# Six modulation vectors of two layers: from matrix products to sums of products along rows

## The chip, the cores and the metric

The kernel runs on one core of a Trainium2 chip. The metric is the device time of one launch in microseconds. The engines are named as the profile names them: PE is TensorE (PEld its weight loads), DVE is VectorE, ACT is ScalarE, POOL is GpSimd, and SP is SyncE, which only issues DMAs here.

## What is computed

Two blocks follow each other. The first has two layers of a mixer (window attention, forgetting attention, a state-space part) and an attention to a memory; the second has two layers of another mixer and a mixture of experts, both modulated by a condition. Only the making of that modulation changes:

```python
def _adaln(cond, w, b):
    return jnp.matmul(jax.nn.silu(cond), w) + b

def _modulate(h, shift, scale):
    return h * (1 + scale) + shift

# second block, layer l of 2; c is [1, 1024], c_ctx [1024], w_mod[l] [1024, 6144]
m_lat = jnp.split(_adaln(c, w_mod[l], b_mod[l])[:, None, :], N_MOD, axis=-1)   # N_MOD = 6
m_ctx = jnp.split(_adaln(c_ctx, w_mod[l], b_mod[l]), N_MOD, axis=-1)
h = _modulate(_rmsnorm(x, norm1_w[l]), m_lat[0], m_lat[1])
```

So for two conditions and two layers a vector of 1024 numbers is multiplied by a matrix of 1024 x 6144 floats, 24 MB a layer. Neither the conditions nor the weights depend on anything that the kernel computes: the work can be done at any time before the second block needs it.

## The kernel before

Features lie on the 128 partitions, tokens along the row. A weight tile of 128 output columns and 1024 inputs is loaded by SP into `wr` (two buffers), split into a high and a low half by ACT (L460, `wh`) and DVE (L462, `wl`, three buffers each), and multiplied in three passes on PE (L472 to L474, into `psg`, two banks). `steps` (L506) runs the tiles of one matrix and hands each result to a callback; after each tile it calls `aside`.

Layer l of the first block is `mixer1` (46 tiles of the input matrix and 16 of the output matrix, between them the scores, softmaxes, convolution and state space) and `memory1` (32 tiles). The trace has layer 0 up to 709 us and layer 1 up to 1450 us; the second block follows.

The modulation is a side line, `adaln`, a generator that `aside` advances. `mixer1` starts it behind its window attention (L736), once in each layer, for that layer's weights; every second tile advances it by two. A step loads 512 KB of weights into `wm` (two buffers of 4 KB a partition) and issues four matmuls on PE, whose stationary operand is silu of the two conditions, padded to 32 columns (`cs`, made in `consts2`), each into another strip of 32 rows of the bank `psa`. After sixteen steps ACT copies the bank (L1078), PE transposes it (L1081) and DVE adds the bias into `mod` (L1082). A layer has 48 steps.

A scheduler orders the instructions of each engine: it takes what is ready by its own estimate of time, in the order of the program where several are ready, and gives out the buffers. Each engine then runs its queue in order and waits at semaphores. An instruction that waits holds up all that stands behind it on its engine.

Of the kernel before, what the change touches and what calls it, by code (L numbers as in the profile page):

```python
# [16 lines left out]
OP = mybir.AluOpType  # L17
# [3 lines left out]
P = 128  # L21
# [163 lines left out]
def _layout2(g, A, vec, cst):  # L185
# [1 line left out]
    cst.update(d)  # L187
    A.update(cp)
    A["ctx_in"] = g["ctx_2"][0]
    vec["cc"] = np.ascontiguousarray(  # L190
        np.stack([_cols(g["c_2"][0]), _cols(g["c_ctx_2"])], 2).reshape(P, 16))
    lb = g["hg_lb_logits_2"]
    vec["lbl"] = np.concatenate([_cols(lb[d_, l]) for l in range(2) for d_ in range(2)], 1)
    for l in range(DEPTH):
# [6 lines left out]
        A[f"v_o{l}0"] = _pieces(g["w_out_2"][l][:384], 2)  # L201
        A[f"v_o{l}1"] = _pieces(g["w_out_2"][l][768:], 2)
        A[f"v_o{l}2"] = _pieces(g["w_out_2"][l][384:768], 2)
        A[f"wm{l}"] = np.ascontiguousarray(
            g["w_mod_2"][l].reshape(8, P, 3, 4, 2, 256).transpose(2, 4, 0, 1, 3, 5).reshape(48, P, 1024))
        A[f"rpb{l}"] = _rpb(g["na_rpb_2"][l])
        wr = np.concatenate([g["w_router_2"][l], np.zeros((D, 16), w.dtype)], 1)
        A[f"wr{l}"] = np.ascontiguousarray(wr.reshape(KT, P, 32).transpose(1, 0, 2).reshape(P, -1))
# [26 lines left out]
class _K:  # L235
    def __init__(self, ctx, tc, A, off, boff):
        self.tc, self.nc, self.A = tc, tc.nc, A
        self.n = self.ns = 0
        self.off, self.boff = off, boff
        self.packs = {}  # L240
        self.queue, self.early = [], []
        self.side, self.due = iter(()), 0
        e = ctx.enter_context
        self.pools = {"one": e(tc.tile_pool(name="p_one", bufs=1)),
                      "y": e(tc.tile_pool(name="p_y", bufs=8, reuse_waits="tile"))}
        self.ps = e(tc.tile_pool(name="ps", bufs=1, space=PSUM))
        self.ps_bufs = {"g": 2, "s": 2, "t": 2, "o": 1, "a": 1}
# [245 lines left out]

    def aside(self):

        self.due += 1
        if self.due % 2 == 0:
            for _ in range(2):
                next(self.side, None)

    def until(self, g):

# [85 lines left out]
    def mixer1(self, l, x, ps, rb):  # L588
# [144 lines left out]
            vec.scalar_tensor_tensor(y, po, 0.5, ga[j], OP.mult, OP.mult)  # L733
            y0.append(self.hilo(y, "y"))

        self.side = self.adaln(l)  # L736

        kq = []

# [298 lines left out]
    def consts2(self):  # L1038
        nc, A = self.nc, self.A
        self.hm = self.one("hm", [P, 5 * 32], U8)  # L1040
        hm = self.tl("t", [P, 512])[:, :5 * 32]
        nc.sync.dma_start(hm, A["hmask"])
        nc.vector.tensor_copy(self.hm, hm)

        cc = self.v("cc").rearrange("p (k v) -> p k v", v=2)
        th = self.sm("cth", [P, 8, 2])
        nc.scalar.activation(th, cc, AF.Tanh, scale=0.5)
        hc = self.sm("chf", [P, 8, 2])
        nc.vector.tensor_scalar(hc, cc, 0.5, None, OP.mult)
        self.cs = self.one("cs", [P, 8, 32])  # L1050
        nc.vector.memset(self.cs, 0.0)
        nc.vector.scalar_tensor_tensor(self.cs[:, :, :2], th, 1.0, hc, OP.add, OP.mult)

        lbl = self.v("lbl")
        self.lb = self.one("lb", [P, 2, 6])
        nc.vector.tensor_tensor(self.lb[:, 0], lbl[:, :6], lbl[:, 6:], OP.subtract)
        nc.vector.tensor_tensor(self.lb[:, 1], lbl[:, 6:], lbl[:, :6], OP.subtract)
        nc.scalar.activation(self.lb, self.lb, AF.Exp)
        nc.vector.tensor_scalar(self.lb, self.lb, BIG, 1.0, OP.min, OP.add)
        nc.vector.reciprocal(self.lb, self.lb)  # L1060
        self.mod = [self.one(f"mod{l}", [P, 6, 8, 2]) for l in range(DEPTH)]

    def adaln(self, l):

        nc = self.nc
        bm = self.v(f"bm{l}")
        for s in range(3):
            ps = self.pt("a")
            for n in range(16):
                hf, k = n // 8, n % 8  # L1070
                raw = self.tl("wm", [P, 1024])
                nc.sync.dma_start(raw, self.A[f"wm{l}"][s * 16 + n])
                for j in range(4):
                    nc.tensor.matmul(ps[32 * j:32 * j + 32, hf * 256:hf * 256 + 256], self.cs[:, k],
                                     raw[:, j * 256:(j + 1) * 256], start=k == 0, stop=k == 7)
                yield
            row = self.tl("t", [P, 512])
            nc.scalar.activation(row, ps, AF.Copy)  # L1078
            pq = self.pt("a")
            for b in range(4):  # L1080
                nc.tensor.transpose(pq[:, b * P:(b + 1) * P], row[:, b * P:(b + 1) * P], self.idf)  # L1081
            nc.vector.tensor_tensor(  # L1082
                self.mod[l][:, 2 * s:2 * s + 2].rearrange("p m (h b) v -> p (m h) b v", h=2),
                pq.rearrange("p (b j r) -> p j b r", b=4, j=4)[:, :, :, :2],
                bm[:, 16 * s:16 * s + 16].rearrange("p (j b) -> p j b", j=4)[:, :, :, None].to_broadcast([P, 4, 4, 2]),
                OP.add)

    def mod_cols(self, l, v, n, w):

# [743 lines left out]
def tile_body(ctx, tc, A, off, boff, out):  # L1833
# [3 lines left out]
    K.consts()  # L1837
    x = K.one("x", [P, KT, T])
    cx = K.one("cx", [P, KT, 256])
    with K.scope(wr=2, wh=3, wl=3, t=6, tg=3, h=16, f2=24, ac=2, xc=2, wm=2, sm=2, s1=1):  # L1840
        ss = K.s1("ssx", [P, 8])
        K.to_feat(A["x"], 4, x, "f2", ss)
        K.consts1()
        nc.vector.tensor_tensor(ss[:, :4], ss[:, :4], ss[:, 4:], OP.add)
        rb = K.row_of(K.rsqrt(ss[:, :4], 4, 1.0 / D), 4)
        K.consts2()
        ps = None
        for l in range(DEPTH):
            mT, ps = K.mixer1(l, x, ps, rb)
# [1 line left out]
                K.to_feat(A["ctx_in"], 2, cx, "f2")  # L1851
            rb = None
            (ps, *pw), hcT = K.memory1(l, x, mT, ps, cx)
            for _ in K.side:
                pass
        rb = K.final_norm([ps, *pw]), hcT
    K.block2(x, cx, rb, dram, out)

# [19 lines left out]
```

## Time and profile before

| | us |
|---|---|
| median of three runs (lowest to highest) | 3010.46 (3009.3 to 3012.07) |
| the profiled execution | 3010.19 |
| its span, first to last instruction | 3007.3 |
| PE busy in the span | 2794.3 |
| DVE, ACT, POOL busy | 1532.0, 1198.2, 278.6 |

Times of rows count from the start of the span. Busy time is the time in which at least one instruction of an engine runs; its instructions overlap a little at their ends, so the durations of single instructions add up to somewhat more. A row of groups gives line, engine, operation, tiles and shape, count, busy us, mean ns, and the idle time ahead of it with what ended that. Tiles are named by the program without their numbers: `wl<-wr,wh` writes `wl` from `wr` and `wh`.

### The profile page before, as it was taken

The numbers are of one execution on the slowest core, as the hardware profiler recorded it, in microseconds if no ns is written. First come the engines' busy times: TensorE is split into PE (matmuls) and PEld (weight loads), VectorE is DVE, ScalarE is ACT, GpSimd is POOL, SyncE is SP. The second block draws the span as 40 slices with busy tenths as digits, with TensorE's granted clock in tenths as the row PEclk, the third lists the DMA queues.
The fourth block names the chain that finished last, engine by engine and source line by source line (L and its number), as shares of the span: only waits on it lengthen the run. The fifth ranks groups of instructions, "written<-read, shape, count | busy, mean of one in ns | idle before, by whom it ended". The sixth has DMA issues, their size and how long they took to land. (4 is left out here: it accounts for less than half of the span.)

```text
span 3007.3 us, 46731 instructions
## 1 busy us (share of the span) xinstructions
PE 2794.3 (93%) x18975; PEld 1932.1 (64%) x18976; DVE 1532.0 (51%) x3103; ACT 1198.2 (40%) x2466; POOL 278.6 (9%) x276
## 2 busy tenths in 40 slices
PE   7999999999999999999999999989996999997975
PEld 5777767876777767877776877733334767773321
DVE  4655786544565686636456556721115365574100
ACT  4545354443554454434455243331112463443110
POOL 0000031000100030100011011011111010001101
PEclk9999999999999999999999999989997999998999
DMA  4232425412222424421110110589974111129997
GB/s 135 64 133 92 168 99 175 152 59 70 77 99 106 140 97 163 167 93 40 54 39 22 58 44 27 226 338 378 372 287 121 63 34 55 52 73 358 409 404 301
DMA packets 97574, 439.53 MB, mean 146 GB/s; under 512 B 11216, under 2 KB 12496, under 8 KB 72784
## 3 DMA queue, kind: packets, MB, share of 16 engines
q1 hardware_dynamic: 86976, 401.09, 36.2%
q0 software_dynamic: 9520, 32.32, 4.0%
q8 instruction: 149, 2.44, 0.3%
q10 hardware_dynamic: 864, 3.15, 0.3%
q14 instruction: 65, 0.53, 0.1%
HBM read 416.40 MB, written 20.97 MB: 145 GB/s over the span
## 5 line engine op out<-in xcount | busy, mean ns | idle before, releaser
L472 PE MATMUL psg<-h,wh 128*128 128x512 f32 x1616 | 652.0, 404 | 2.4 <-ACT z L1345 1.9
L474 PE MATMUL psg<-h,wl 128*128 128x512 f32 x1616 | 646.2, 400 | 0.0
L473 PE MATMUL psg<-h,wh 128*128 128x512 f32 x1616 | 644.3, 399 | 0.0
L462 DVE TENSOR_TENSOR wl<-wr,wh 128x1024 fp32r<-128x1024 f32 (+2 forms) x272 | 339.9, 1250 | 432.9 <-ACT wh L460 418.2
L460 ACT ACTIVATE wh<-wr 128x1024 fp32r<-128x1024 f32 (+2 forms) x272 | 280.8, 1033 | 515.1 <-PE psg L473 440.8
L472 PEld LDWEIGHTS psg<-h,wh 128*128 128x128 f32 x1616 | 305.6, 189 | 88.9 <-issue 20.7
L474 PEld LDWEIGHTS psg<-h,wl 128*128 128x128 f32 x1616 | 305.5, 189 | 71.5 <-issue 9.8
L473 PEld LDWEIGHTS psg<-h,wh 128*128 128x128 f32 x1616 | 305.6, 189 | 68.1 <-issue 7.9
L1750 PE MATMUL psg<-ew,xg 128*64 128x512 f32 x832 | 221.6, 605 | 23.0 <-DMA ew<-in_eu_dram 12.2
L472 PE MATMUL psg<-y,wh 128*128 128x256 f32 (+1 forms) x560 | 182.1, 326 | 1.3 <-ACT y L448 0.6
L473 PE MATMUL psg<-y,wh 128*128 128x256 f32 (+1 forms) x560 | 181.1, 324 | 1.9 <-DVE y L449 1.9
L474 PE MATMUL psg<-y,wl 128*128 128x256 f32 (+1 forms) x560 | 180.0, 323 | 0.2 <-DVE wl L462 0.2
L1750 PEld LDWEIGHTS psg<-ew,xg 128*64 128x64 f32 x832 | 65.0, 138 | 154.4 <-issue 112.1
L472 PEld LDWEIGHTS psg<-y,wh 128*128 128x128 f32 x560 | 108.7, 195 | 15.1 <-DVE x L1101 2.0
L472 PE MATMUL psg<-f,wh 128*128 128x256 f32 (+1 forms) x360 | 113.2, 316 | 4.0 <-DVE x L582 1.8
L473 PEld LDWEIGHTS psg<-y,wh 128*128 128x128 f32 x560 | 108.4, 194 | 11.5 <-DVE y L449 2.2
L1030 ACT ACTIVATE t<-pst 128x512 f32<-128x512 f32 (+1 forms) x134 | 69.6, 557 | 110.9 <-PE pst L1027 110.6
L473 PE MATMUL psg<-f,wh 128*128 128x256 f32 (+1 forms) x360 | 112.8, 314 | 0.8 <-DVE f L1265 0.8
L474 PEld LDWEIGHTS psg<-y,wl 128*128 128x128 f32 x560 | 108.8, 195 | 6.6 <-issue 0.6
L474 PE MATMUL psg<-f,wl 128*128 128x256 f32 (+1 forms) x360 | 111.6, 310 | 0.0
L1777 PE MATMUL pss<-ew,hid 128*64 128x512 f32 x400 | 106.3, 597 | 4.2 <-DMA ew<-in_ed_dram 4.2
L1027 PE MATMUL pst<-const_sb,t 128*128 128x128 f32 x488 | 83.3, 280 | 6.3 <-DVE t L1255 4.5
(475 smaller groups left out, 4525.5 us busy)
## 6 DMA issues: line engine op xcount, KB each, us to landing
ew<-in_eg_dram SPq DMA_DIRECT2D x52, 1024.0 KB, 15.0
ew<-in_eu_dram SPq DMA_DIRECT2D x52, 1024.0 KB, 9.8
ew<-in_ed_dram SPq DMA_DIRECT2D x50, 1024.0 KB, 10.2
wm<-in_wm_dram SPq DMA_DIRECT2D x96, 512.0 KB, 4.1
wr<-in_w_f_dram SPq DMA_DIRECT2D x92, 512.0 KB, 3.6
wr<-in_v_f_dram SPq DMA_DIRECT2D x60, 512.0 KB, 3.3
wr<-in_w_o_dram SPq DMA_DIRECT2D x32, 512.0 KB, 5.0
x<-in_ed_dram SPq DMA_DIRECT2D x10, 1024.0 KB, 16.8
```

The costliest lines, as they stand in the source:

```text
L460: nc.scalar.activation(hi, raw, AF.Copy)
L462: nc.vector.tensor_tensor(lo, raw, hi, OP.subtract)
L472: t.matmul(ps, a[0], b[0], start=first, stop=False)
L473: t.matmul(ps, a[0], b[1], start=False, stop=False)
L474: t.matmul(ps, a[1], b[0], start=False, stop=last)
L1027: ten.transpose(pp[:, (2 * i + a) * P:(2 * i + a + 1) * P], ps[a][:, c:c + P], self.idf)
L1030: self.nc.scalar.activation(pT[:, :w], pp[:, :w], AF.Copy)
L1750: ten.matmul(ps[e * 64:(e + 1) * 64], x0[:, d, e * 64:(e + 1) * 64], wn[e][:, k], start=d == 0, stop=d == 7)
L1777: ten.matmul(ps[e * 64:(e + 1) * 64], hid[0, q][:, f, e * 64:(e + 1) * 64], w[j][e][:, f], start=f == 0, stop=f == 3)
```

## The change

The weights of the modulation are transposed on the host: 48 tiles a layer, in which a partition holds one output and the row half of its 1024 weights (512 floats, 256 KB a tile). The two conditions are stored 128 times over, once for each partition. `adaln` now runs once, over both layers. For each half it loads the conditions (`csb`) and makes their silu with ACT and GpSimd. A step loads one tile into `wm` (three buffers of 2 KB, for the tile `w` and for a product `q`); GpSimd multiplies it by the silu of the second condition into `q`, ACT sums `q` along the row, and DVE multiplies by the first condition, over `w` itself, and sums in one instruction. The sums land in `part`; DVE adds the halves and the bias at the end of a layer's second half. There are 192 steps; `aside` advances one at every tile, from the first tile of layer 0 on. The pool `f2` of feature tiles has 23 buffers instead of 24. PE, its bank `psa` and the transposes are not used by the modulation any more.

```diff
--- before.py
+++ after.py
@@ -187,8 +187,7 @@
     cst.update(d)
     A.update(cp)
     A["ctx_in"] = g["ctx_2"][0]
-    vec["cc"] = np.ascontiguousarray(
-        np.stack([_cols(g["c_2"][0]), _cols(g["c_ctx_2"])], 2).reshape(P, 16))
+    A["cc"] = _bc(np.stack([g["c_2"][0], g["c_ctx_2"]], 0).reshape(2, 2, 512).transpose(1, 0, 2).reshape(-1))
     lb = g["hg_lb_logits_2"]
     vec["lbl"] = np.concatenate([_cols(lb[d_, l]) for l in range(2) for d_ in range(2)], 1)
     for l in range(DEPTH):
@@ -201,8 +200,7 @@
         A[f"v_o{l}0"] = _pieces(g["w_out_2"][l][:384], 2)
         A[f"v_o{l}1"] = _pieces(g["w_out_2"][l][768:], 2)
         A[f"v_o{l}2"] = _pieces(g["w_out_2"][l][384:768], 2)
-        A[f"wm{l}"] = np.ascontiguousarray(
-            g["w_mod_2"][l].reshape(8, P, 3, 4, 2, 256).transpose(2, 4, 0, 1, 3, 5).reshape(48, P, 1024))
+        A[f"wm{l}"] = np.ascontiguousarray(g["w_mod_2"][l].T.reshape(48, P, 2, 512).transpose(2, 0, 1, 3))
         A[f"rpb{l}"] = _rpb(g["na_rpb_2"][l])
         wr = np.concatenate([g["w_router_2"][l], np.zeros((D, 16), w.dtype)], 1)
         A[f"wr{l}"] = np.ascontiguousarray(wr.reshape(KT, P, 32).transpose(1, 0, 2).reshape(P, -1))
@@ -239,7 +237,7 @@
         self.off, self.boff = off, boff
         self.packs = {}
         self.queue, self.early = [], []
-        self.side, self.due = iter(()), 0
+        self.side = iter(())
         e = ctx.enter_context
         self.pools = {"one": e(tc.tile_pool(name="p_one", bufs=1)),
                       "y": e(tc.tile_pool(name="p_y", bufs=8, reuse_waits="tile"))}
@@ -493,10 +491,7 @@
 
     def aside(self):
 
-        self.due += 1
-        if self.due % 2 == 0:
-            for _ in range(2):
-                next(self.side, None)
+        next(self.side, None)
 
     def until(self, g):
 
@@ -733,7 +728,6 @@
             vec.scalar_tensor_tensor(y, po, 0.5, ga[j], OP.mult, OP.mult)
             y0.append(self.hilo(y, "y"))
 
-        self.side = self.adaln(l)
 
         kq = []
 
@@ -1042,15 +1036,6 @@
         nc.sync.dma_start(hm, A["hmask"])
         nc.vector.tensor_copy(self.hm, hm)
 
-        cc = self.v("cc").rearrange("p (k v) -> p k v", v=2)
-        th = self.sm("cth", [P, 8, 2])
-        nc.scalar.activation(th, cc, AF.Tanh, scale=0.5)
-        hc = self.sm("chf", [P, 8, 2])
-        nc.vector.tensor_scalar(hc, cc, 0.5, None, OP.mult)
-        self.cs = self.one("cs", [P, 8, 32])
-        nc.vector.memset(self.cs, 0.0)
-        nc.vector.scalar_tensor_tensor(self.cs[:, :, :2], th, 1.0, hc, OP.add, OP.mult)
-
         lbl = self.v("lbl")
         self.lb = self.one("lb", [P, 2, 6])
         nc.vector.tensor_tensor(self.lb[:, 0], lbl[:, :6], lbl[:, 6:], OP.subtract)
@@ -1060,30 +1045,33 @@
         nc.vector.reciprocal(self.lb, self.lb)
         self.mod = [self.one(f"mod{l}", [P, 6, 8, 2]) for l in range(DEPTH)]
 
-    def adaln(self, l):
+    def adaln(self):
+
 
         nc = self.nc
-        bm = self.v(f"bm{l}")
-        for s in range(3):
-            ps = self.pt("a")
-            for n in range(16):
-                hf, k = n // 8, n % 8
-                raw = self.tl("wm", [P, 1024])
-                nc.sync.dma_start(raw, self.A[f"wm{l}"][s * 16 + n])
-                for j in range(4):
-                    nc.tensor.matmul(ps[32 * j:32 * j + 32, hf * 256:hf * 256 + 256], self.cs[:, k],
-                                     raw[:, j * 256:(j + 1) * 256], start=k == 0, stop=k == 7)
-                yield
-            row = self.tl("t", [P, 512])
-            nc.scalar.activation(row, ps, AF.Copy)
-            pq = self.pt("a")
-            for b in range(4):
-                nc.tensor.transpose(pq[:, b * P:(b + 1) * P], row[:, b * P:(b + 1) * P], self.idf)
-            nc.vector.tensor_tensor(
-                self.mod[l][:, 2 * s:2 * s + 2].rearrange("p m (h b) v -> p (m h) b v", h=2),
-                pq.rearrange("p (b j r) -> p j b r", b=4, j=4)[:, :, :, :2],
-                bm[:, 16 * s:16 * s + 16].rearrange("p (j b) -> p j b", j=4)[:, :, :, None].to_broadcast([P, 4, 4, 2]),
-                OP.add)
+        part = self.s1("adp", [P, DEPTH, 2, 2, 48])
+        for h in range(2):
+            cs = self.s1("csb", [P, 2, 512])
+            nc.sync.dma_start(cs, self.A["cc"][:, h * 1024:(h + 1) * 1024].rearrange("p (v k) -> p v k", v=2))
+            for v in range(2):
+                th = self.tl("wm", [P, 512])
+                nc.scalar.activation(th, cs[:, v], AF.Tanh, scale=0.5)
+                nc.gpsimd.tensor_tensor(th, th, cs[:, v], OP.mult)
+                nc.gpsimd.tensor_tensor(th, th, cs[:, v], OP.add)
+                nc.scalar.activation(cs[:, v], th, AF.Copy, scale=0.5)
+            for l in range(DEPTH):
+                for n in range(48):
+                    w, q = self.tl("wm", [P, 512]), self.tl("wm", [P, 512])
+                    nc.sync.dma_start(w, self.A[f"wm{l}"][h, n])
+                    nc.gpsimd.tensor_tensor(q, w, cs[:, 1], OP.mult)
+                    nc.scalar.activation(q, q, AF.Copy, accum_out=part[:, l, h, 1, n:n + 1])
+                    nc.vector.tensor_tensor_reduce(w, w, cs[:, 0], 1.0, 0.0, OP.mult, OP.add, part[:, l, h, 0, n:n + 1])
+                    yield
+                if h:
+                    m = self.mod[l].rearrange("p m k v -> p v (m k)")
+                    bm = self.v(f"bm{l}")[:, None, :].to_broadcast([P, 2, 48])
+                    nc.vector.tensor_tensor(m, part[:, l, 0], part[:, l, 1], OP.add)
+                    nc.vector.tensor_tensor(m, m, bm, OP.add)
 
     def mod_cols(self, l, v, n, w):
 
@@ -1837,13 +1825,14 @@
     K.consts()
     x = K.one("x", [P, KT, T])
     cx = K.one("cx", [P, KT, 256])
-    with K.scope(wr=2, wh=3, wl=3, t=6, tg=3, h=16, f2=24, ac=2, xc=2, wm=2, sm=2, s1=1):
+    with K.scope(wr=2, wh=3, wl=3, t=6, tg=3, h=16, f2=23, ac=2, xc=2, wm=3, sm=2, s1=1):
         ss = K.s1("ssx", [P, 8])
         K.to_feat(A["x"], 4, x, "f2", ss)
         K.consts1()
         nc.vector.tensor_tensor(ss[:, :4], ss[:, :4], ss[:, 4:], OP.add)
         rb = K.row_of(K.rsqrt(ss[:, :4], 4, 1.0 / D), 4)
         K.consts2()
+        K.side = K.adaln()
         ps = None
         for l in range(DEPTH):
             mT, ps = K.mixer1(l, x, ps, rb)
@@ -1851,8 +1840,8 @@
                 K.to_feat(A["ctx_in"], 2, cx, "f2")
             rb = None
             (ps, *pw), hcT = K.memory1(l, x, mT, ps, cx)
-            for _ in K.side:
-                pass
+        for _ in K.side:
+            pass
         rb = K.final_norm([ps, *pw]), hcT
     K.block2(x, cx, rb, dram, out)
```

What the scheduler makes of it differs from the order in the program. DVE at the first output matrix of layer 0, before (L582 adds a result to `x`, L462 makes a low half):

```order
L462 TENSOR_TENSOR wl_1775<-wr_1771,wh_1773 128x1024
L582 TENSOR_TENSOR x<-x,psg_1697 128x512
L582 TENSOR_TENSOR x<-x,psg_1711 128x512
L462 TENSOR_TENSOR wl_1964<-wr_1960,wh_1962 128x1024
L582 TENSOR_TENSOR x<-x,psg_1731 128x512
L582 TENSOR_TENSOR x<-x,psg_1745 128x512
L462 TENSOR_TENSOR wl_2019<-wr_2015,wh_2017 128x1024
```

The same place on DVE now (L460 is the low half, L577 the addition, L1068 the product and its sum, two instructions):

```order
L460 TENSOR_TENSOR wl_2047<-wr_2043,wh_2045 128x1024
L1068 ISA wm_4098,adp_381<-wm_4098,csb_382 128x512
L1068 ISA adp_381 128x1
L577 TENSOR_TENSOR x<-x,psg_1814 128x512
L1068 ISA wm_4138,adp_381<-wm_4138,csb_382 128x512
L1068 ISA adp_381 128x1
L577 TENSOR_TENSOR x<-x,psg_1828 128x512
L460 TENSOR_TENSOR wl_2096<-wr_2092,wh_2094 128x1024
```

Two products stand between one low half and the next, each ahead of an addition. Counted over the whole order, 16 products stand ahead of the twelfth of the 272 low halves, 80 between that and the 45th, none up to the 48th, 39 up to the 72nd, 52 up to the 96th and 5 behind it; the 94th is the last of layer 0. In the trace of before the 12th, 45th, 48th, 72nd and 96th start at 92, 369, 416, 565 and 709 us.

PE at the same output matrix, before (L1074 are the matmuls of the modulation):

```order
L473 MATMUL psg_1651<-y_1457,wh_1647 128x512
L474 MATMUL psg_1651<-y_1456,wl_1649 128x512
L1074 MATMUL psa_1503<-wm_1679,cs 32x256 x4
L1074 MATMUL psa_1503<-wm_1685,cs 32x256
L472 MATMUL psg_1665<-y_970,wh_1647 128x512
L473 MATMUL psg_1665<-y_971,wh_1647 128x512
```

And now, between the first and the second result of that matrix:

```order
L471 MATMUL psg_1734<-y_1541,wh_1730 128x512
L472 MATMUL psg_1734<-y_1540,wl_1732 128x512
L566 MATMUL pss_1894<-f_368_1578,f_376_1625 128x128
L470 MATMUL psg_1748<-y_1036,wh_1730 128x512
L471 MATMUL psg_1748<-y_1037,wh_1730 128x512
L472 MATMUL psg_1748<-y_1036,wl_1732 128x512
```

The matmuls of the modulation are gone from the row of the others; one of the scores (L566) stands there.

## Rows read from the trace of the kernel before

**Rows 1.** The page: busy us, share of the span and instructions by engine.
```profile
PE 2794.3 (93%) x18975; PEld 1932.1 (64%) x18976; DVE 1532.0 (51%) x3103; ACT 1198.2 (40%) x2466; POOL 278.6 (9%) x276
```

**Rows 2.** Windows: length; PE, PEld, DVE, ACT, POOL busy (records); clock, DMA, GB/s.
```profile
92.00:369.00 277.00, 273.39 (x1658) 202.79 (x1658) 178.53 (x377) 133.73 (x299) 8.58 (x21) 1.00 0.34 116
369.00:416.00 47.00, 43.72 (x342) 31.31 (x342) 43.80 (x83) 27.20 (x72) 15.14 (x13) 1.00 0.20 70
416.00:565.00 149.00, 146.94 (x926) 116.88 (x927) 104.59 (x174) 69.23 (x122) 19.52 (x14) 1.00 0.46 157
565.00:709.00 144.00, 141.17 (x695) 112.43 (x694) 57.65 (x108) 56.76 (x126) 0.00 (x0) 1.00 0.29 94
625.00:677.00 52.00, 49.73 (x203) 34.09 (x202) 25.50 (x77) 24.24 (x79) 0.00 (x0) 1.00 0.12 41
709.00:1240.00 531.00, 513.41 (x3016) 378.60 (x3015) 336.63 (x633) 250.08 (x515) 50.20 (x51) 0.99 0.33 112
```

**Rows 3.** Waits from 92 to 565 us: total, times, longest, of two engines.
```profile
DVE wl L462 <- ACT wh L460: 46.8, 36, 4.9
...
ACT wh L460 <- PE psg L473: 84.0, 40, 5.6
```

**Rows 4.** Windows of the modulation's matmuls (tile wm) alone: length; PE, PEld busy.
```profile
92.00:369.00 277.00, 16.83 (x224) 6.19 (x224) 1.00 0.34 116
369.00:416.00 47.00, 2.75 (x32) 0.96 (x32) 1.00 0.20 70
416.00:565.00 149.00, 9.18 (x128) 3.46 (x128) 1.00 0.46 157
709.00:1240.00 531.00, 30.40 (x384) 10.68 (x384) 0.99 0.33 112
```

**Rows 5.** Timeline of TensorE around one group: start, duration, line.
```profile
170.38 1.07 PE L1074 MATMUL psa<-wm,cs 128*32 128x256 f32 x16
171.38 0.50 PE L472 MATMUL psg<-h,wh 128*128 128x512 f32 x1
```

**Rows 6.** Groups of DVE from 92 to 565 us: busy us, mean ns, idle before.
```profile
L863 DVE SCALAR_TENSOR_TENSOR f<-f,f 128x512 f32<-128x512 f32 x8 | 5.5, 690 | 0.2
L826 DVE TENSOR_TENSOR t<-t,t 128x512 f32<-128x512 f32 x16 | 15.2, 951 | 0.4 <-ACT t L825 0.2
L855 DVE TENSOR_TENSOR f<-f,ends 128x512 f32<-128x512 f32 x4 | 4.6, 1147 | 0.0
L828 DVE COPY ends<-t 128x4 f32<-128x4 f32 x16 | 5.7, 354 | 0.0
```

**Rows 7.** Groups of GpSimd from 92 to 565 us.
```profile
L830 POOL TENSOR_TENSOR t<-t,f 128x512 f32<-128x512 f32 x12 | 17.6, 1467 | 23.7 <-ACT t L825 8.6 <-DVE ends L828 8.5 <-ACT wh L460 5.4
L875 POOL TENSOR_TENSOR x<-x,tg 128x512 f32<-128x512 f32 x8 | 10.3, 1291 | 93.0 <-DVE tg L874 93.0
L846 POOL TENSOR_TENSOR t<-f,dst 128x512 f32<-128x512 f32 x6 | 6.7, 1121 | 11.7 <-PE pso L839 6.3 <-PE pss L849 3.0 <-DVE f L801 2.4
```

**Rows 8.** Timelines of GpSimd and of DVE at one place.
```profile
499.80 1.29 POOL L875 TENSOR_TENSOR x<-x,tg 128x512 f32<-128x512 f32 x1 [5.75 <-DVE tg L874]
...
499.94 2.23 DVE L462 TENSOR_TENSOR wl<-wr,wh 128x1024 fp32r<-128x1024 f32 x1 [0.23 <-ACT wh L460]
```

**Rows 9.** Lines of DVE with min/median/max ns; the mean of one of them.
```profile
L462 DVE TENSOR_TENSOR wl<-wr,wh x272: 681/1226/2351, 19.4 to 2710.2; 128x1024 fp32r<-128x1024 f32 x124, 128x768 fp32r<-128x768 f32 x8, 128x512 fp32r<-128x512 f32 x4
...
L828 DVE COPY ends<-t x32: 154/164/952, 371.7 to 1131.9; 128x4 f32<-128x4 f32 x32
...
L462 DVE TENSOR_TENSOR wl<-wr,wh 128x1024 fp32r<-128x1024 f32 x61 | 82.3, 1349 | 48.7 <-ACT wh L460 46.8 <-PE pst L799 0.8 <-PE psg L474 0.6
```

**Rows 10.** Groups of ACT to 60 us: a square with its sum, and the sum's read.
```profile
L360 ACT ACTIVATE tg<-f 128x512 f32<-128x512 f32 x8 | 5.0, 621 | 4.3 <-DMA f<-in_x_dram 4.3
L360 ACT ACTIVATION_READ_ACCUMULATOR tg<-f 128x1 f32 x8 | 1.5, 190 | 0.0
```

**Rows 11.** DMA issues: KB each, median us to landing.
```profile
wr<-in_v_o_dram SPq DMA_DIRECT2D x8, 256.0 KB, 2.5
```

## The prediction

> **What bounds the kernel now.** I read the page first, then the windows of the two layers of the first block, then the single rows. TensorE is busy 93% of the span [rows 1]. [...] Next comes DVE: 178.53 + 43.80 + 104.59 = 327 of 473 us (69%), in the 47 us from 369 to 416 already 43.80 (93%) [rows 2]. Its longest wait is for the high halves of the weights, 46.8 us, and ACT waits 84.0 us for TensorE to give those buffers back [rows 3]. That idle time is prefetch held back by a full buffer, so it can absorb some work, not all. GpSimd works 43 us there [rows 2]. From 1240 us on nothing is touched.
>
> **What leaves TensorE.** The 768 records of the modulation lie half in each layer and cover 28.76 us (16.83 + 2.75 + 9.18) and 30.40 us [rows 4]. Against one group: its 16 records start at 170.38, the matmul behind them at 171.38 us; 48 groups of 1.00 us are 48 us [rows 5]. So 48 to 59 us leave TensorE; I take 59, which has the switches in it and the groups that are split. The 24 transposes behind them, at the 0.06 us of one record, are 1.5 us; I leave them out.
>
> **Where the new work lands.** It doesn't stay where the old was. The order puts 16 of the 192 steps ahead of the twelfth low half of the weights (92 us in the trace), 80 from there to 369, none to 416, 39 to 565, 52 to 709 and 5 later. Layer 1 thus loses its modulation and gets nothing for it, while layer 0 takes nearly all.
>
> **DVE in layer 0.** A 128x512 product of two SBUF tensors takes 0.69 us [rows 6]. The read of its sum lies between nothing and the 0.164 us of the smallest copy [rows 9]; part of it lies beside the next product. I take 0.7 us a step: 178.53 + 80 x 0.7 = 234.5 us in the 277 us to 369, 43.8 in the next 47, 104.59 + 39 x 0.7 = 131.9 in the 149 to 565 [rows 2]. TensorE without its modulation would want 260, 44 and 140 us [rows 2, 4]. By this alone DVE still fits, at 90 to 99%.
>
> **What GpSimd takes from DVE.** This decides. A two-tensor product of 128x512 takes GpSimd 1.29 us [rows 7]. At 499.80 us one starts, and the DVE subtraction that starts at 499.94 takes 2.23 us, where 1.226 is its median [rows 8, 9]. So a DVE instruction that reads two SBUF tensors stands while GpSimd reads two. [...] From the rows: 61 subtractions at 1349 instead of 1226 ns make 7.5 us over eight L875 products, 0.94 us each [rows 7, 9]. Beside the 18 products of L830 and L846, DVE lost (951-690) x 16 + (1147-690) x 4 + (354-164) x 16 = 9.0 us, 0.5 each [rows 6, 7, 9]. The new rows stand nearer to the first: the product of DVE overwrites the weights that GpSimd reads, so it waits for GpSimd, and the subtractions behind it stand in the same queue. I take 0.7, with 0.5 and 0.94 as ends. To 369 that is 234.5 + 56 = 290.5 us (274.5 to 309.7) for 277; to 565 131.9 + 27.3 = 159.2 (151.4 to 168.6) for 149. Sum with the 47: 497 for 473, +24 us (0 to +52).
>
> DVE never runs without gaps: its fullest stretch is 93% busy [rows 2]. At 93%, 290.5 becomes 312 and 159.2 becomes 171, +58 us (+32 to +88). I take the middle between no gap and that, **+40 us in layer 0** instead of the 29 it should have gained. Queued behind a late product on DVE are the low halves, the softmax steps and the additions that free TensorE's PSUM buffers, so TensorE waits for what stands behind it.
>
> **The rest.** From 565 to 709 us DVE has 57.65 us [rows 2]; 52 x 1.4 = 73 fit. Only the softmax of the memory from 625 to 677 is dense: 25.50 + 20 x 1.4 = 53.5 us for 52 [rows 2]. I put +3 us (0 to +8). ACT gets 0.62 + 0.19 us a step [rows 10], at most 119 x 0.81 = 96 us on 133.73 + 27.20 + 69.23 = 230 of 473 [rows 2]: 69%, hidden by its waits for TensorE's buffers, and if those are gone its sums come late and hold the buffer of the next step. SP issues 192 loads of 256 KB where it issued 96 of 512 KB; the same bytes; 256 KB need 2.5 us to land [rows 11]. They wait for a buffer ahead of the loads of the weights, but two steps need 2.5 + 1.29 + 0.81 us, 4.6, and have eight (473/119 each). On GpSimd the products and casts of the attention now stand behind new ones that wait for their load; with 119 x 1.29 + 43 = 197 of 473 us it is free more than half of the time, so I charge nothing, up to 1.29 us at each of its 26 products, those of DVE's waits above among them [rows 2, 7]. One buffer fewer in the pool of features: no row shows a wait on it; I take nothing, up to 6 us as for the longest wait on a weight buffer, 5.6 [rows 3].
>
> **Sum.** Layer 0 +40 and +3, layer 1 -30: +13 us on the profiled 3010.2 us, **3023 us**; the median 3010.46 is the same to 0.3 us. Its own range is 2983 (0.5 us a product, no gaps) to 3080 (0.94 us at 93%, the softmax at +8, layer 1 at 26 instead of 30).
>
> **Rivals.**
> *The cover holds.* DVE's waits for the high halves shrink instead, and the products of GpSimd fall where DVE waits anyway. From 0.3 us a product downwards (234.5 + 80 x 0.3 = 258.5 under the 260 of TensorE) most of layer 0's 29 us comes too: 3010 - 59 = 2951 in full, 2980 if layer 0 only breaks even. For it: DVE has 146 us of idle time, and its longest total of waits is for buffers that are full [rows 3]. Against it: no stretch of DVE above 93%. 31%.
> *The fused sum is slow.* No row of this trace multiplies and sums on DVE. Bounds are 0.69 us, a plain product, and 1.23 us, the subtraction of twice the width [rows 6, 9]. At 1.23, 119 x 0.54 = 64 us more in a layer where DVE has no room: 3087, up to 3130 with 0.94 us. For it speaks only that the sum is one more thing to do; the plain product of that width costs 0.69. 12%. [...]
> *Layer 1 gives nothing*, because what TensorE then waits for takes the place: DVE is at 336.63 of 531 us there [rows 2], so I give it 7%, at 3040 to 3053.
>
> The forecast has 50%. Of it some 9 in 50 lie within 0.2% (6 us, about what a measurement of this kernel can tell from no change) and 3 below; of the first rival three in 31 lie within. So faster 0.31, same 0.12, slower 0.57. The range leaves out the fullest form of the first rival (2951 to 2960) and the end of the second: 2960 to 3095.
>
> **What would show it.** Subtractions (the low halves) with a mean over 1.5 us in layer 0; products of DVE waiting for GpSimd; TensorE idle for 40 to 80 us between 92 and 620 us in place of 9, with waits on DVE; layer 1 some 30 us shorter than its 531. Wrong: TensorE as full as before in layer 0 and that layer shorter (cover), fused products over 1 us (second rival), or layer 1 as long as before.

## The result and the profile after

The changed kernel takes **3066.44 us** (median of four runs, 3062.84 to 3069.0) against 3011.24 (3009.3 to 3012.07) in the same comparison: a ratio of 1.0179, 95% interval 1.0166 to 1.0191. The forecast was 3023 in a range from 2960 to 3095, slower at 57%. The sign and the ranges hold; the loss is 55 us (56 between the spans of the profiled executions) where the sum had 13.

Lines of the changed kernel are two to twelve lower than before: L460 makes the low half (L462 before), L458 the high half, L470 to L472 multiply. New are L1066 (GpSimd's product), L1067 (ACT's sum) and L1068 (DVE's product and sum). The page's row of busy time and instructions, to be held against [rows 1]:

```profile
PE 2754.6 (90%) x18184; PEld 1919.1 (63%) x18184; DVE 1743.2 (57%) x3482; ACT 1321.6 (43%) x2851; POOL 575.4 (19%) x476
```

Windows of the changed kernel from the 12th to the 72nd low half, on to the 96th, and to the 160th (length; PE, PEld, DVE, ACT, POOL busy; granted clock, DMA, GB/s). The same pieces of work were 92 to 565, 565 to 709 and 709 to 1241 us before, [rows 2] but for 1 us:

```profile
99.00:623.00 524.00, 450.81 (x2529) 347.18 (x2528) 455.78 (x857) 306.84 (x729) 232.31 (x172) 0.97 0.40 125
623.00:788.00 165.00, 147.84 (x702) 115.96 (x701) 112.27 (x216) 90.49 (x230) 70.97 (x53) 0.97 0.52 164
788.00:1296.00 508.00, 480.73 (x2617) 369.17 (x2617) 342.80 (x647) 250.63 (x523) 54.24 (x56) 0.97 0.21 71
```

The first stretch begins 7 us later and takes 524 us for 473, the memory's 165 for 144, layer 1 takes 508 for 532: +7 + 51 + 21 - 24, and 1 us more behind that. TensorE, idle for 9 us in the first stretch before, is idle for 73. It waits less for DVE (33 us in all) than for ACT (40). Waits of TensorE from 99 to 623 us (total, times, longest):

```profile
PE pss L811 <- ACT t L804: 12.0, 2, 10.0
PE psg L470 <- ACT xc L771: 8.8, 6, 2.0
PE pst L1021 <- DVE t L1009: 7.8, 9, 1.6
PE pst L362 <- ACT cx L366: 7.2, 2, 6.8
```

ACT in turn waits for GpSimd, and so does DVE. Waits of ACT and of DVE in the same stretch; before, the longest of ACT was 84.0 us, for TensorE to free a weight buffer, and that of DVE 46.8 us, for ACT's high halves [rows 3]:

```profile
ACT wm L1067 <- POOL wm L1066: 83.3, 67, 3.7
ACT wh L458 <- PE psg L471: 21.9, 13, 6.4
```

```profile
DVE wm L1068 <- POOL wm L1066: 32.9, 27, 3.2
DVE wl L460 <- ACT wh L458: 11.6, 15, 3.1
```

Of the prefetch that had been held back by full buffers little is left: 21.9 us of ACT's 84.0, 11.6 of DVE's 46.8. The new operations themselves cost what the rows of before gave for their like (min, median and max ns of DVE's product, of the read of its sum, of GpSimd's product):

```profile
L1068 DVE CUSTOM_DVE_ANT_0 wm<-wm,csb x192: 674/690/1787, 35.4 to 812.6; 128x512 f32<-128x512 f32 x192
L1068 DVE DVE_READ_ACCUMULATOR2_ANT adp<- x192: 72/80/86, 36.0 to 813.2; 128x1 f32 x192
```

```profile
L1066 POOL TENSOR_TENSOR wm<-wm,csb x192: 1262/1298/2382, 29.1 to 800.3; 128x512 f32<-128x512 f32 x192
```

The maxima show the two engines in each other's way. DVE and then GpSimd at one place of the convolution (start, us, engine, line; in brackets the wait ahead of it):

```profile
345.55 1.79 DVE L779 SCALAR_TENSOR_TENSOR f<-tg,tg 128x512 f32<-128x512 f32 x1
347.26 0.54 DVE L773 TENSOR_SCALAR tg<-xc,cvh 128x512 f32<-128x512 f32 x1
347.72 1.77 DVE L1068 CUSTOM_DVE_ANT_0 wm<-wm,csb 128x512 f32<-128x512 f32 x1
```

```profile
344.76 2.03 POOL L1066 TENSOR_TENSOR wm<-wm,csb 128x512 f32<-128x512 f32 x1
347.62 1.32 POOL L1066 TENSOR_TENSOR wm<-wm,csb 128x512 f32<-128x512 f32 x1 [0.83 <-ACT wm L1067]
```

L779 is an operation like L863 of [rows 6], which takes 0.69 us on two tensors of 128x512. Here it begins while GpSimd multiplies and takes 1.79. The product that begins 0.10 us behind GpSimd's takes 1.77.

### The profile page after: what moved, and what is told of

Its sections match the earlier page's. It is cut to its first block, busy times and chain, and to the rows that moved or that the text cites. A ratio compares the mean times of both kernels' runs of the same rounds, so it can differ in the third digit from the quotient of the medians.

```text
span 3063.7 us, 46567 instructions
## 1 busy us (share of the span) xinstructions
PE 2754.6 (90%) x18184; PEld 1919.1 (63%) x18184; DVE 1743.2 (57%) x3482; ACT 1321.6 (43%) x2851; POOL 575.4 (19%) x476
## 5 line engine op out<-in xcount | busy, mean ns | idle before, releaser
L470 PE MATMUL psg<-h,wh 128*128 128x512 f32 x1616 | 652.0, 404 | 15.1 <-ACT xc L771 8.1
L471 PE MATMUL psg<-h,wh 128*128 128x512 f32 x1616 | 648.5, 401 | 3.2 <-DVE h L862 2.6
L472 PE MATMUL psg<-h,wl 128*128 128x512 f32 x1616 | 649.1, 402 | 0.0
L460 DVE TENSOR_TENSOR wl<-wr,wh 128x1024 fp32r<-128x1024 f32 (+2 forms) x272 | 351.5, 1293 | 322.9 <-ACT wh L458 315.7
L458 ACT ACTIVATE wh<-wr 128x1024 fp32r<-128x1024 f32 (+2 forms) x272 | 280.3, 1031 | 347.9 <-PE psg L471 292.7
L470 PEld LDWEIGHTS psg<-h,wh 128*128 128x128 f32 x1616 | 307.8, 191 | 95.9 <-issue 10.5
L471 PEld LDWEIGHTS psg<-h,wh 128*128 128x128 f32 x1616 | 307.4, 190 | 74.7 <-issue 10.9
L472 PEld LDWEIGHTS psg<-h,wl 128*128 128x128 f32 x1616 | 307.4, 190 | 69.5 <-issue 8.5
L1066 POOL TENSOR_TENSOR wm<-wm,csb 128x512 f32<-128x512 f32 x192 | 278.8, 1452 | 362.2 <-DMA wm<-in_wm_dram 205.2
L1068 DVE CUSTOM_DVE_ANT_0 wm<-wm,csb 128x512 f32<-128x512 f32 x192 | 156.7, 819 | 78.7 <-POOL wm L1066 78.6
L1067 ACT ACTIVATE wm<-wm 128x512 f32<-128x512 f32 x192 | 121.2, 632 | 175.7 <-POOL wm L1066 165.2
L470 PE MATMUL psg<-y,wh 128*128 128x256 f32 (+1 forms) x560 | 182.7, 327 | 8.4 <-ACT wh L458 4.4
L471 PE MATMUL psg<-y,wh 128*128 128x256 f32 (+1 forms) x560 | 182.1, 326 | 1.9 <-DVE y L447 1.9
L472 PE MATMUL psg<-y,wl 128*128 128x256 f32 (+1 forms) x560 | 182.2, 326 | 1.3 <-DVE wl L460 1.3
L470 PEld LDWEIGHTS psg<-y,wh 128*128 128x128 f32 x560 | 109.3, 196 | 19.9 <-ACT wh L458 4.8
L470 PE MATMUL psg<-f,wh 128*128 128x256 f32 (+1 forms) x360 | 113.1, 316 | 5.6 <-DVE x L577 1.8
L471 PEld LDWEIGHTS psg<-y,wh 128*128 128x128 f32 x560 | 108.8, 195 | 12.4 <-issue 2.6
L472 PEld LDWEIGHTS psg<-y,wl 128*128 128x128 f32 x560 | 109.5, 196 | 8.2 <-DVE wl L460 1.6
L471 PE MATMUL psg<-f,wh 128*128 128x256 f32 (+1 forms) x360 | 112.6, 313 | 0.8 <-DVE f L1253 0.8
L472 PE MATMUL psg<-f,wl 128*128 128x256 f32 (+1 forms) x360 | 111.4, 310 | 0.9 <-DVE wl L460 0.9
```

The costliest lines, as they stand in the source:

```text
L458: nc.scalar.activation(hi, raw, AF.Copy)
L460: nc.vector.tensor_tensor(lo, raw, hi, OP.subtract)
L470: t.matmul(ps, a[0], b[0], start=first, stop=False)
L471: t.matmul(ps, a[0], b[1], start=False, stop=False)
L472: t.matmul(ps, a[1], b[0], start=False, stop=last)
L1066: nc.gpsimd.tensor_tensor(q, w, cs[:, 1], OP.mult)
```

## The experiments

Each kernel is an edit of the changed one; all have its loads and its order of aside steps, as the scheduler then arranges them. Times are medians; the intervals of the ratios are some 0.17% (5 us) to either side, and the kernel before was at 3008.9 to 3011.1 us in these comparisons. What the expectations call a lock is a DVE instruction that takes longer beside one of GpSimd, as in [rows 8]: 2.23 us for a median of 1.226.

**What do the loads cost, and what did TensorE give back?**

```diff
-                    nc.gpsimd.tensor_tensor(q, w, cs[:, 1], OP.mult)
-                    nc.scalar.activation(q, q, AF.Copy, accum_out=part[:, l, h, 1, n:n + 1])
-                    nc.vector.tensor_tensor_reduce(w, w, cs[:, 0], 1.0, 0.0, OP.mult, OP.add, part[:, l, h, 0, n:n + 1])
```

> The steps of the modulation load their 192 tiles and nothing else: the product of GpSimd, the sum of ACT and the product of DVE are left out, so both conditions get the bias alone. What TensorE gave up is gone as in the changed kernel. If all of the loss comes from the products and their waits, this shows the whole relief: 3010 - 59 = 2951 us (to 2960), and TensorE at a granted clock of 1.00 from 92 to 565 us. If the loads on SP's queue or the one buffer fewer of the features cost something, it stays above 2965.

2962.57 us, ratio 0.9838 (0.9821 to 0.9854), between the two ranges. The relief is 48 us, at the low end of the 48 to 59, with what the loads and the missing buffer may take off it.

**DVE's products alone**: the first two of those lines are left out, the third stays.

> GpSimd's product and ACT's sum are left out (the second condition gets the bias alone); DVE keeps its 192 products. Nothing can stand for GpSimd here, neither by a lock nor by a wait. By the theory that DVE's load decides (0.77 us a product, 119 of them between the 12th and the 45th low half: 178.5 + 92 = 270 us for the 260 that TensorE wants, some 290 at 93%), layer 0 gives back part of its relief: 2965 to 3000 us, near 2985. By the rival, that what costs is the waiting of DVE and ACT for GpSimd, nothing is left of it: 2951 to 2960. The difference to the changed kernel's 3066 is the price of GpSimd's half.

2961.37 us, ratio 0.9831 (0.9814 to 0.9847). Without GpSimd's half, DVE's 192 products are free; by the theory of my prediction they should have cost some 24 us. Two windows of this kernel, in the part of layer 0 between the 12th and the 45th low half, where the products stand closest:

```profile
308.00:357.00 49.00, 49.00 (x227) 40.65 (x226) 49.00 (x94) 19.97 (x29) 0.91 (x9) 1.00 0.63 202
143.00:196.00 53.00, 51.81 (x311) 39.01 (x308) 50.35 (x138) 31.25 (x83) 4.63 (x4) 1.00 0.55 179
```

DVE is busy for 49.00 of 49 us, and TensorE is too. The whole stretch from the 12th to the 72nd low half takes 454 us, with loads alone 452.

**GpSimd and ACT alone**: the third line is left out.

> DVE's product is left out (the first condition gets the bias alone); GpSimd multiplies and ACT sums as in the changed kernel. If the loss is DVE's load, only the lock of 0.7 us a product of GpSimd is left on DVE: 234.5 us of the 260 that TensorE wants to the 45th low half, 2955 to 2975 us, with the low halves still slowed to a mean near 1.4 us. If it is the waiting of ACT for GpSimd (165 us over the changed kernel), which holds up the high halves, it is still there: 3000 to 3040 us.

3046.29 us, ratio 1.0117 (1.0100 to 1.0134). So 84 of the 104 us that the steps cost (3066 - 2963) are here, without any product on DVE. It stands above the range of the rival, too.

**The steps spread evenly** over both layers.

```diff
-                    w, q = self.tl("wm", [P, 512]), self.tl("wm", [P, 512])
+                    wq = self.tl("wl", [P, 1024])
+                    w, q = wq[:, :512], wq[:, 512:]
...
-    with K.scope(wr=2, wh=3, wl=3, t=6, tg=3, h=16, f2=23, ac=2, xc=2, wm=3, sm=2, s1=1):
+    with K.scope(wr=2, wh=3, wl=5, t=6, tg=3, h=16, f2=23, ac=2, xc=2, wm=1, sm=2, s1=1):
```

> All of the changed kernel's work, but each step takes its two buffers from the ring of the low halves (five tiles of 4 KB instead of three, no buffers of its own but one), so that the order can't draw the steps together: 33 instead of 80 between the 12th and the 45th low half, 23 instead of 39 to the 72nd, 24 instead of 52 to the 96th, the rest in layer 1. If the loss comes from DVE having no room where the steps lie close, DVE has 178.5 + 33 x 1.47 = 227 us in the 260 of TensorE, 104.6 + 34 = 138 in 140, and in layer 1 some 402 in 501: 2955 to 2995 us, near 2975. If each step costs the same wherever it stands (3066 - 2951 = 115 us over 192 steps, 0.6 each), the time stays at 3050 to 3070.

3040.30 us, ratio 1.0099 (1.0082 to 1.0116): between the two. Drawing the steps together, with the buffers that this goes with, costs 26 of 104 us; the rest is paid wherever they stand. Layer 1 takes as long as before in this kernel (535 us for 532, 504 with loads alone): what TensorE gave up there is eaten by the steps.

**GpSimd's product alone**, the second and third line left out:

> DVE's product and ACT's sum are left out (both conditions get the bias alone); GpSimd's 192 products stay. Loads alone took 2963 us, products of DVE alone 2961, GpSimd with ACT's sums 3046, so the price lies in GpSimd's half. If it is the lock that GpSimd's product with two tensors puts on DVE, or the work of the attention that queues behind it on GpSimd, it is all still here: 3020 to 3050 us. If it is ACT, whose sums wait for GpSimd while the high halves stand behind them, it is gone: 2961 to 2975.

3035.72 us, ratio 1.0085 (1.0068 to 1.0102). This is 11 us below the kernel with ACT's sums, and the two intervals overlap; the sums' own share isn't settled.

**ACT's sums alone**, on the loaded weights, `nc.scalar.activation(w, w, AF.Copy, accum_out=...)`:

> GpSimd's and DVE's products are left out (both conditions come out wrong); ACT sums the loaded weights as they are, 192 times 0.63 + 0.19 us, and waits for no engine but the load. If ACT's own time were the price (138 of the sums stand between the 12th and the 45th low half, 112 us on 134 in 277), this would take 3000 us or more. If it is the waiting for GpSimd or GpSimd's lock, it takes 2961 to 2975.

2960.92 us, ratio 0.9839 (0.9823 to 0.9856). ACT's time is free, too. What is left is GpSimd, and the next four take it apart. All leave DVE's product out.

**A short instruction in the same place of the queue**, without ACT's sum:

```diff
-                    nc.gpsimd.tensor_tensor(q, w, cs[:, 1], OP.mult)
+                    nc.gpsimd.tensor_scalar(q[:, :4], w[:, :4], 0.5, None, OP.mult)
```

> GpSimd's instruction of each step is kept with its wait for the load and its place in the queue, but multiplies 4 columns by a constant instead of 512 by the silu; DVE's product and ACT's sum are left out (both conditions get the bias alone). If the price is that the attention's own work on GpSimd stands behind instructions that wait for a load (GpSimd waited 150 us for loads between 92 and 560 us with its products alone), most of the 73 us that GpSimd's products alone cost over the loads is still here: 3000 to 3036. If it is the time in which GpSimd works, by its lock on DVE or by its own length, it is gone: 2960 to 2972.

2960.76 us, ratio 0.9841 (0.9824 to 0.9858). That GpSimd's queue stands for loads has no price: it waits 355 us for them, against 243 with the product.

**Its full length, one tensor read**: `nc.gpsimd.tensor_scalar(q, w, 0.5, None, OP.mult)`.

> As the kernel before this one, in the same order, but with all 512 columns: GpSimd multiplies by a constant, one tensor read (both conditions get the bias alone). Against GpSimd's products of two tensors alone (3036) this takes away the reading of the second tensor, against the 4 columns it adds GpSimd's time, some 1.68 us each. If the lock is the price, 2965 to 2985 us; if GpSimd's time is it, 3005 to 3025.

2986.48 us, ratio 0.9928 (0.9909 to 0.9947). Against the 4 columns 26 us are lost; the second tensor adds 49. The lock's range is missed by 1.5 us, less than the interval, that of GpSimd's time by 19. The 49 us don't come from GpSimd's own length: its instruction that reads one tensor is the longer one (median 1493 ns to 1297). Nor do they come from the order: in the three kernels with 4 columns, one tensor and two, DVE does its work in the same order, but for two instructions from one kernel to the next. What the second tensor does to DVE is in the page's rows of loads alone, of one tensor and of two, with the same 3099 instructions of DVE:

```profile
PE 2731.6 (92%) x18184; PEld 1912.8 (65%) x18184; DVE 1532.5 (52%) x3099; ACT 1196.8 (40%) x2467; POOL 285.9 (10%) x284
```

```profile
PE 2734.7 (92%) x18183; PEld 1912.0 (64%) x18184; DVE 1556.2 (52%) x3099; ACT 1195.3 (40%) x2467; POOL 609.8 (20%) x476
```

```profile
PE 2756.2 (91%) x18183; PEld 1926.5 (63%) x18184; DVE 1624.6 (54%) x3099; ACT 1195.3 (39%) x2467; POOL 572.0 (19%) x476
```

DVE's own work grows by 24 us beside 192 instructions that read one tensor (0.12 each), by 92 beside those that read two (0.48 each).

**The same, with the attention's and convolution's work taken from GpSimd to DVE** (six lines of the first block, of which two):

```diff
-            pool.memset(u_[:, :3], 0.0)
+            vec.memset(u_[:, :3], 0.0)
...
-            pool.tensor_tensor(x[:, f], x[:, f], t, OP.add)
+            vec.tensor_tensor(x[:, f], x[:, f], t, OP.add)
```

> As the kernel before this one, but the attention's and convolution's own work on GpSimd in the first block is on DVE, so that nothing waits for GpSimd but the modulation's buffers (both conditions get the bias alone). If what the steps delay is that work, in GpSimd's queue, the time falls to that of the loads alone and a little for DVE's 30 us more a layer: 2963 to 2980 us. If GpSimd slows DVE while it works, it stays where the kernel before this one is, or goes above it.

2962.97 us, ratio 0.9844 (0.9828 to 0.9861). But not all of the 24 us is a queue relieved. Windows from the 12th to the 72nd low half and from the 96th to the 160th, with one tensor on GpSimd's queue beside the other work, and then without that work:

```profile
93.00:561.00 468.00, 441.30 (x2524) 344.76 (x2523) 343.00 (x618) 228.43 (x491) 296.11 (x201) 0.98 0.47 154
708.00:1211.00 503.00, 481.70 (x2632) 370.17 (x2632) 335.49 (x635) 246.35 (x512) 46.87 (x51) 0.98 0.20 69
```

```profile
89.00:549.00 460.00, 437.25 (x2525) 341.20 (x2524) 355.21 (x666) 229.43 (x492) 261.20 (x156) 0.99 0.49 160
695.00:1192.00 497.00, 481.06 (x2639) 369.78 (x2639) 343.18 (x689) 247.14 (x513) 0.00 (x0) 0.99 0.20 70
```

Up to the 72nd low half 12 us go (561 to 549), where the steps are; 6 more go in layer 1, where there is no step at all. There GpSimd was late with the kernel's own work, which DVE does sooner. These two profiled executions are 16 us apart, the medians 24. And the same six lines gain about as much where GpSimd has no step: in the kernels with both conditions on DVE, further down, the 72nd low half comes 9 us sooner for them (541 to 532) and layer 1 takes 8 us less (501 to 493). So the queue explains between some 3 and 12 of the 26 us. No run has these lines with the loads alone, which would settle it.

**One tensor, with ACT's sums**: GpSimd's line is `nc.gpsimd.tensor_scalar(q, w, 0.5, None, OP.mult)` again, and ACT's line behind it stays.

> As GpSimd with ACT's sums (DVE's product left out), but GpSimd multiplies the weights by a constant, so that it reads one tensor and not two (the second condition comes out wrong). ACT still waits for GpSimd, and GpSimd's queue is as long. If the price is that DVE stands while GpSimd reads two tensors, it is gone: 2961 to 2980 us, and the low halves and the other subtractions of DVE are back at their means of before. If it is the waiting of ACT, or GpSimd's queue, it stays: 3025 to 3050.

3021.09 us, ratio 1.0040 (1.0027 to 1.0054), in neither range. Below the 3046 with two tensors, far above the 2986 without the sums: with one tensor ACT's sums cost 35 us, with two some 11. The costs don't add up, and the orders of the kernels with and without the sums differ; how ACT's waiting for GpSimd (97 us in this kernel) and the time that GpSimd takes from DVE share the loss stays open.

**Both conditions on DVE**, the whole computation without GpSimd's products and ACT's sums:

```diff
-                    nc.gpsimd.tensor_tensor(q, w, cs[:, 1], OP.mult)
-                    nc.scalar.activation(q, q, AF.Copy, accum_out=part[:, l, h, 1, n:n + 1])
+                    nc.vector.tensor_tensor_reduce(q, w, cs[:, 1], 1.0, 0.0, OP.mult, OP.add, part[:, l, h, 1, n:n + 1])
```

> The whole computation, with both conditions on DVE: two products with their sums a step, 384 times 0.69 + 0.08 = 296 us, no GpSimd, no sum on ACT. Products of DVE alone cost nothing, though DVE was busy to 95 of 100 where they lay. 110 steps' worth of two conditions' products (of 384) lie between the 12th and the 45th low half: 178.5 + 85 = 263 us in the 265 that this stretch took with loads alone, 94 up to the 96th: 58 + 72 = 130 in 144. If DVE's time has no price while it fits, 2961 to 2985 us, faster than both kernels; if DVE is the bound once it is full, 3000 to 3030.

2957.74 us, ratio 0.9824 (0.9807 to 0.9840): 109 us below the change and 3 below what I expected, and the whole relief of TensorE is kept. The order puts the steps that don't fit into the memory's part and into layer 1. The stretch from the 12th to the 72nd low half, and layer 1:

```profile
89.00:541.00 452.00, 433.73 (x2532) 342.69 (x2531) 415.09 (x941) 229.69 (x491) 56.10 (x52) 0.99 0.37 122
687.00:1188.00 501.00, 479.96 (x2631) 369.40 (x2631) 395.90 (x839) 246.31 (x511) 50.81 (x51) 0.98 0.28 95
```

**And the first block's other work on GpSimd as well**, the six lines of above:

> The whole computation with both conditions on DVE, as in the kernel that took 2958, and the attention's and convolution's own work on GpSimd in the first block is on DVE too, so GpSimd does next to nothing up to the second block. DVE is the fullest that the first block can make it: 0 to 700 us had it busy for 603 us, and some 30 us come on top in each layer. If DVE's time has no price as long as the order can place it where DVE is free, and the queue of GpSimd still costs a little (layer 1 was 7 us shorter without it), 2945 to 2957 us. If DVE is now the bound in places, 2960 to 2990.

2941.82 us, ratio 0.9772 (0.9758 to 0.9786), faster than both kernels and 3 us below what I expected. The page's row, and the same two stretches:

```profile
PE 2726.9 (93%) x18184; PEld 1908.2 (65%) x18184; DVE 1764.7 (60%) x3972; ACT 1194.4 (41%) x2467; POOL 191.3 (7%) x178
```

```profile
87.00:532.00 445.00, 434.67 (x2530) 342.58 (x2529) 406.13 (x961) 227.02 (x487) 0.00 (x0) 0.99 0.35 119
677.00:1170.00 493.00, 476.97 (x2629) 366.02 (x2628) 413.81 (x938) 245.64 (x511) 0.00 (x0) 0.99 0.31 102
```

Over the span DVE is at its fullest of all kernels here, in the first stretch at 406 of 445 us (91%, after 92% in the kernel before this one), and TensorE is idle for 10 us there, less than with loads alone (18).

## Why the prediction was right in its sign and wrong in its size

| what the steps do | us |
|---|---|
| nothing (kernel before) | 3011 |
| load | 2963 |
| and 4 columns on GpSimd | 2961 |
| and 512 columns on GpSimd, one tensor read | 2986 |
| and 512 columns, two tensors | 3036 |
| and ACT's sums | 3046 |
| and DVE's products (the change) | 3066 |

**What leaves TensorE.** Before, TensorE was busy for 464 of the 473 us from 92 to 565 us [rows 2], and what left it became time: 59 was taken, 48 came. The 48 whole groups at 1.00 us came nearer than the windows' sum. Most of the gap is in layer 0: with loads alone its end, the 96th low half, comes at 688 us for 709, some 22 us sooner where 29 were counted; layer 1 takes 504 for 532, 28 of the 30, and 3 us are given back behind it. The 24 transposes, left out at 0.06 us each, last 0.27 us each in the trace and cover 3.9 us.

**Where the work lands.** As the order said: all but five of the steps stand ahead of the 96th low half, and layer 1 became 24 us shorter, for the 30 of the sum.

**DVE's product.** The 0.7 us were right: 0.69, and 0.08 for the read that lies in part beside the next. The second rival is out; it had one in eight. The fused product, a custom operation in the trace, has a median of 690 ns, and L863, a product of the same size without a sum, a mean of 690 [rows 6].

**The step that failed is the next one**: that DVE's busy time turns into the kernel's time, as soon as it exceeds 93% of what TensorE leaves. It charged DVE's own products and the time that GpSimd takes from DVE alike. The stretch from the 12th to the 72nd low half, with loads alone, with 4 columns on GpSimd and with GpSimd's products of two tensors alone, contradicts it:

```profile
91.00:543.00 452.00, 434.01 (x2517) 342.51 (x2516) 322.25 (x618) 229.05 (x491) 47.09 (x52) 0.99 0.49 162
91.00:539.00 448.00, 431.36 (x2516) 339.98 (x2515) 319.50 (x618) 228.36 (x490) 109.75 (x200) 1.00 0.48 162
95.00:612.00 517.00, 457.49 (x2519) 355.60 (x2518) 396.67 (x618) 228.04 (x490) 264.41 (x198) 0.95 0.42 140
```

DVE's products alone make it busy for 91% of this stretch (411 of 454 us, below), in places for 49.00 of 49 us, and cost nothing. GpSimd's products alone leave it at 77% (397 of 517 us; 74% from the 12th to the 45th low half, a piece that takes 305 us for 269 with loads alone), and the kernel is 73 us longer than with loads alone, 49 of it by the second tensor. Added DVE time has no one price: 110 us of its own products cost nothing, 24 us that GpSimd's one-tensor instructions add go with 26 us of the kernel over the 4 columns, 92 us that the two-tensor ones add with 75. As I read it, the order knows of DVE's products and puts them where DVE is free; time that GpSimd takes isn't in the order: it falls on whatever DVE is at, and a subtraction or a softmax step that TensorE waits for is late by it. No run shows that reason by itself. Nor are DVE's products free beside GpSimd's: with them there, they wait for GpSimd, and the kernel goes from 3046 to 3066 us. The first rival, that the cover holds, was right of DVE's half and wrong of GpSimd's, whose price it wanted below 0.3 us.

**What GpSimd takes from DVE.** 0.7 us a product was taken, 0.5 to 0.94 as ends. Measured are 0.48 (92 us over 192), and 0.53 in the changed kernel (1743.2 us of DVE against 1642.3 with its products alone): the low end, that of L830 and L846, was the nearer row. It goes as [rows 8] showed it (a subtraction of 2.23 us for 1.226), and the reading of [rows 6] holds: without any work on GpSimd in the first block, in the last kernel, L820, L849 and L822 (L826, L855 and L828 before) take 689, 688 and 163 ns for 951, 1147 and 354. So the +40 in layer 0 against 51 measured came about, by luck, of two errors that nearly met: too much for DVE's products, too little for what GpSimd's cost.

**The rest.** Here more than half of the miss lies, 25 of the 43 us between +13 and +56. The memory's part was given +3 and took +21, the start 0 and took +7. GpSimd's queue was charged with nothing, in the sentence on its products and casts; it is worth some 3 to 12 us of the 26 that one-tensor instructions cost. ACT's sums were called hidden by the waits for weight buffers, with the remark that they come late if those are gone. They went, from 84 us to 21.9. The loads, SP's queue and the buffer fewer of the features were charged with nothing, and the loads-only kernel agrees to within the 11 us that the relief falls short of 59.

**The clock**, which no term had. From 92 to 709 us the clock was 1.00 before [rows 2]. In the changed kernel it is 0.97 from 99 to 623 us, where TensorE is idle for 73 us, and 0.95 with GpSimd's products alone, where it is idle for 60. Of pieces of 20 us of the changed kernel it is lowest in that from 399 to 419 us, at 0.74, where TensorE was busy for 9.74 of 20 us. In each us from 403 to 412 it is 0.50 there, from 413 on 1.00; a matmul of 128x512 on L471 takes 0.63 us at 410.32 and 0.39 at 413.37. The same matmuls keep TensorE busy for 450.81 us, for 434.51 with DVE's products alone:

```profile
92.00:546.00 454.00, 434.51 (x2521) 341.91 (x2520) 411.31 (x943) 229.87 (x491) 52.86 (x52) 0.99 0.51 168
```

Of the 70 us between the two, 54 are idle time and 16 busier TensorE, most of it by the clock (3% of 524 us less 1% of 454 are 11 us, my estimate).

**What would show it.** TensorE's idle time (73 us in 40 to 80) and DVE's waits for GpSimd came as said. The low halves' mean over 1.5 us came in the memory's part alone (1632 ns over 24), 1391 ns over the 61 from 99 to 623 us, and the waits of TensorE are on ACT more than on DVE.

## What to carry to other kernels

Before an engine is charged with added work, ask whether the order can place it: work of low urgency in an engine's own queue was free here with that engine busy for 91% of a stretch, while work on another engine that takes time out of its instructions was not. A product of two tensors on GpSimd isn't free help for DVE: per product it took 0.48 us from DVE, whose own product with sum needs 0.77. Moving the second condition's products and sums to the fuller engine gained 109 us here, and the rest of the first block's work on GpSimd 16 more.

## What the runs showed of the hardware

GpSimd's product with a constant is slower than that with a tensor (median 1493 to 1297 ns at 128x512), and yet takes a quarter from DVE (0.12 us an instruction to 0.48). Which of the two engines stands can be seen beside it: a DVE subtraction of two tensors that begins first keeps its 1.23 us, and GpSimd's instruction, 0.12 us behind, takes 2.46. The kernel with one tensor, DVE and then GpSimd:

```profile
343.38 1.23 DVE L460 TENSOR_TENSOR wl<-wr,wh 128x1024 fp32r<-128x1024 f32 x1 [0.26 <-ACT wh L458]
```

```profile
343.50 2.46 POOL L1067 TENSOR_SCALAR wm<-wm 128x512 f32<-128x512 f32 x1 [1.45 <-DMA wm<-in_wm_dram]
```

DVE stands, too, when it begins behind a product of two tensors (L1068 of the changed kernel, 0.10 us behind, 1.77 us for a median of 0.69). Behind an instruction that reads one tensor it need not. In the kernel with one tensor, GpSimd and then DVE, which begins 1.01 us behind and keeps the 0.75 us that L775 takes without any work on GpSimd (mean 750 ns in the last kernel):

```profile
321.74 3.11 POOL L1067 TENSOR_SCALAR wm<-wm 128x512 f32<-128x512 f32 x2 [1.14 <-DMA wm<-in_wm_dram]
```

```profile
322.75 0.75 DVE L775 SCALAR_TENSOR_TENSOR tg<-xc,cvh,tg 128x512 f32<-128x512 f32 x1
```

The low halves of this kernel show the same: one that begins 0.09 us behind GpSimd's instruction takes 1.63 us for 1.23, those that begin 0.55 us or more behind it, with 0.66 us or more of it left, take 1.21 to 1.23. Behind GpSimd's products of two tensors, with as much left, they take 1.70 us or more, but for two beside which GpSimd's instruction itself takes 2.4 and 3.1. Whether GpSimd reads one tensor or two is 0.12 us of DVE against 0.48 an instruction here, and 49 us of the kernel.
